# A softmax kernel whose second load is issued as 16 DMAs of unequal partition counts

## The chip, the cores and the metric

The kernel runs on one core of one Trainium2 chip. The metric is the time of the whole program on the device in microseconds (us), the median over runs; lower is better. The span of a profile runs from the first to the last instruction and is about 1.8 us shorter than that. Each experiment was timed on the same chip as a run of the kernel before.

## The reference

```python
x: (16, 1024, 512) float32
def reference(x):
    x_max = np.max(x, axis=-1, keepdims=True)
    exp_x = np.exp(x - x_max)
    return (exp_x / np.sum(exp_x, axis=-1, keepdims=True)).astype(np.float32)
```

It is 33.55 MB in and 33.55 MB out.

## The kernel before

The 16384 rows are cut into ten chunks. Chunk k gives `R` rows to each of the 128 partitions and has a place in one SBUF tile of 96 rows. SyncE issues the loads and ScalarE the stores. VectorE finds the row maxima (reduction) and scales; ScalarE computes the exponentials and their sums. SBUF is the core's on-chip memory, in 128 partitions. A DMA copies between it and DRAM; it *lands* at the last recorded increment of its semaphore, a counter that engines wait for (the trace of the kernel before has 368 increments by DMAs, 16 for each of its 23). In the profile DVE is VectorE, ACT ScalarE, POOL GpSimd, and SPq is SyncE's own list of instructions.

```python
CHUNKS = [
    (3, 0), (5, 3), (8, 8), (16, 16), (16, 32), (16, 48), (16, 64), (16, 80), (16, 0), (16, 16),
]                      # (rows per partition, first SBUF row)
EARLY = 8              # loads 0 to 7 stand first in the program
AFTER_STORE = {2: [8], 3: [9]}
FINISH_BEFORE = (1, 2, 3)
ON_ACT = ()            # loads that ScalarE issues
AT_HEAD = {mybir.EngineType.SP: 1}   # the first load is issued ahead of the start barrier
# ... cut: views, groups of 8 rows ...
    def load(k):
        queue = nc.scalar if k in ON_ACT else nc.sync
        queue.dma_start(out=place[k], in_=src[k])
# ... cut: rowmax and exps ...
    def scale(g):
        # ... cut: reciprocal of the sums, one multiplication per row ...
        if since is not None:
            nc.scalar.dma_start(
                out=dst[k][:, since:b, :], in_=place[k][:, since:b, :]
            )
        if b == CHUNKS[k][0]:
            for later in AFTER_STORE.get(k, ()):
                load(later)
# ... cut ...
        for k in range(EARLY):
            load(k)
        # then per group: rowmax, exps, and the scale of the group before
```

One thing is not in this text. The instruction records of both traces show eight semaphores for these DMAs, numbers 99, 100 and 103 to 108, shared by loads and stores and used in turn: in the trace of the changed kernel the first load has 99, the 16 shares of the second 100, 103, 104, 106, 107, 108, 99, 100, 103, 104, 105, 106, 107, 108, 99, 100, and the first store has the 105 that the first round leaves out, so that the share of 6 gets it after the store. Of the first eight loads, each that gets a used one is recorded with a wait for it: the sixth to eighth in the kernel before. (The stores' records name a wait for VectorE's semaphore, 101, alone.)

Of the kernel before, what the change touches and what calls it, by code (L numbers as in the profile page):

```python
# [1 line left out]

# [4 lines left out]

F32 = mybir.dt.float32
EXP = mybir.ActivationFunctionType.Exp
AX = mybir.AxisListType.X  # L10


CHUNKS = [
    (3, 0), (5, 3), (8, 8), (16, 16), (16, 32), (16, 48), (16, 64), (16, 80), (16, 0), (16, 16),
]
SBUF_ROWS = 96

EARLY = 8
AFTER_STORE = {2: [8], 3: [9]}

GROUP = 8

FINISH_BEFORE = (1, 2, 3)

STORE_ROWS = {3: 8, 4: 8, 5: 8}

ON_ACT = ()

AT_HEAD = {mybir.EngineType.SP: 1}



def loads_at_the_head(nc):

    main, body = nc.main_func.blocks[0], nc.main_func.blocks[1]
    for engine, count in AT_HEAD.items():
        loads = [
            i
            for i in body.instructions
            if i.engine == engine and type(i).__name__ == "InstDMACopy"  # L40
        ][:count]
        barrier = next(
            n
            for n, i in enumerate(main.instructions)
            if i.engine == engine and type(i).__name__ == "InstDrain"
        )
        for load in loads:
            body.instructions.remove(load)
        main.instructions[barrier:barrier] = loads


@with_exitstack
def kernel(
    ctx: ExitStack,
    tc: tile.TileContext,
    x: bass.AP,
    out: bass.AP,
):
    nc = tc.nc
    nc.at_finalize(loads_at_the_head)  # L60
    P = nc.NUM_PARTITIONS

    x_flat = x.flatten_outer_dims()
    out_flat = out.flatten_outer_dims()
    n, d = x_flat.shape
    assert n == P * sum(R for R, _ in CHUNKS)


    src, dst, at = [], [], 0
    for R, _ in CHUNKS:  # L70
        for flat, views in ((x_flat, src), (out_flat, dst)):
            part = flat[at : at + P * R, :]
            views.append(part.rearrange("(p r) d -> p r d", r=R))
        at += P * R

    data = ctx.enter_context(tc.tile_pool(name="data", bufs=1))
    stats = ctx.enter_context(tc.tile_pool(name="stats", bufs=4))
    held = data.tile([P, SBUF_ROWS, d], F32, name="held")
    place = [held[:, s : s + R, :] for R, s in CHUNKS]


    groups = []
    for k, (R, _) in enumerate(CHUNKS):
        m = max(1, round(R / GROUP))
        cuts = [R * i // m for i in range(m + 1)]
        since = 0
        for a, b in zip(cuts, cuts[1:]):
            ends = b == R or b - since >= STORE_ROWS.get(k, R)
            groups.append((k, a, b, since if ends else None))
            since = b if ends else since  # L90
    shift = [None] * len(groups)
    sums = [None] * len(groups)

    def load(k):
        queue = nc.scalar if k in ON_ACT else nc.sync
        queue.dma_start(out=place[k], in_=src[k])

    def rowmax(g):
        k, a, b, _ = groups[g]
        shift[g] = stats.tile([P, b - a], F32, name="shift", tag="shift")  # L100
        nc.vector.reduce_max(  # L101
            out=shift[g], in_=place[k][:, a:b, :], axis=AX, negate=True
        )

    def exps(g):
        k, a, b, _ = groups[g]
        sums[g] = stats.tile([P, b - a], F32, name="sums", tag="sums")
        for r in range(a, b):
            nc.scalar.activation(  # L109
                out=place[k][:, r, :],  # L110
                in_=place[k][:, r, :],
                func=EXP,
                bias=shift[g][:, r - a : r - a + 1],
                scale=1.0,
                accum_out=sums[g][:, r - a : r - a + 1],
            )

    def scale(g):
        k, a, b, since = groups[g]
        recip = stats.tile([P, b - a], F32, name="recip", tag="recip")  # L120
        nc.vector.reciprocal(out=recip, in_=sums[g])  # L121
        for r in range(a, b):
            nc.vector.tensor_scalar_mul(  # L123
                out=place[k][:, r, :],
                in0=place[k][:, r, :],
                scalar1=recip[:, r - a : r - a + 1],
# [9 lines that stand above are left out]
    with tc.manual_schedule():  # L136
        for k in range(EARLY):
            load(k)
        waiting = None
        for g, (k, a, _, _) in enumerate(groups):  # L140
            if waiting is not None and a == 0 and k in FINISH_BEFORE:
                scale(waiting)
                waiting = None
            rowmax(g)
            exps(g)
            if waiting is not None:
                scale(waiting)
            waiting = g
        scale(waiting)


# [1 line left out]
_INS = ['x']  # L153
_OUTS = [((16, 1024, 512), 'float32')]


# [23 lines left out]
```

## Time and profile before

| | before |
|---|---|
| time, median of 2 runs | 162.52 us (161.56 to 163.48) |
| span of the profile | 159.7 us |
| DMA over the span | 67.13 MB, 420 GB/s |
| VectorE busy, ScalarE busy | 78%, 58% |

First, lines of the page of the kernel before. Each digit is the busy share of one fortieth of the span (4.0 us) in tenths, and each number below is that slice's GB/s. The DMA engines are full, or nearly so, from the second slice to the last but one.

```profile
## 2 busy tenths in 40 slices
DVE  0481870799699999999999999999999999762000
...
DMA  7999999899999999999999999999999999999993
GB/s 269 433 464 411 389 447 446 383 412 466 402 441 431 460 435 396 439 418 468 427 414 439 414 484 427 396 447 402 435 439 476 418 402 468 443 402 468 427 410 164
DMA packets 3315, 67.13 MB, mean 420 GB/s; under 512 B 368, under 2 KB 368, under 8 KB 624
```

The same by windows of the kernel before (start and end, length, busy us and instructions (x) of VectorE, ScalarE and GpSimd, granted clock, busy share of the DMA engines, GB/s):

```profile
0.00:5.00 5.00, 0.52 (x1) 0.47 (x1) 0.20 (x4) 1.00 0.81 303
5.00:10.00 5.00, 2.67 (x6) 3.04 (x7) 0.00 (x0) 1.00 0.99 418
10.00:18.00 8.00, 4.27 (x7) 3.63 (x10) 0.00 (x0) 1.00 1.04 430
18.00:32.00 14.00, 8.15 (x12) 5.75 (x16) 0.00 (x0) 1.00 0.99 424
32.00:100.00 68.00, 66.23 (x82) 49.09 (x137) 0.00 (x0) 1.00 1.01 432
```

At 432 GB/s the 67.13 MB take 155 of the 159.7 us, so the DMA engines are the limit: a microsecond in which they have nothing to do is lost unless the end of the kernel had slack, and for DMA it has none by the slices above (8 or 9 tenths from the second to the last but one).

The front of the chain of waits of the kernel before (start us, us, what). It shows the first load landed at 4.46 us and the second reduction following the first scaling at 10.01 us without a wait: the second load was long there.

```profile
0.00 4.46 DMA held<-in_x_dram
4.46 0.02 issue
4.48 1.76 DVE shift L101
...
8.73 1.28 DVE held L123 x3
10.01 2.74 DVE shift L101
```

SyncE's own waits in the first 20 us of the kernel before (waiter and releaser: us in total, times, longest). It waits only for loads:

```profile
SPq L96 <- DMA held<-in_x_dram: 4.3, 2, 2.7
```

### The profile page before, as it was taken

Reading aid. Unit: us, or ns where it says so; the run is one execution under the profiler, and the core shown is the slowest. Engines: PE = TensorE matmul, PEld = TensorE weight load, DVE = VectorE, ACT = ScalarE, POOL = GpSimd, SP = SyncE. Lnnn points to the kernel's source line nnn. Section 1 sums busy time; section 2 is a strip of 40 time slices with the busy share of each in tenths; the row PEclk is TensorE's granted clock in tenths of the full one; section 3 lists DMA queues with packets and bytes.
Section 4 is the critical chain, followed back from the end, with each engine's and each line's share of the span. In section 5 each row is a group of like instructions: output and inputs, shape, how many; then the busy total and the mean of one; then the engine's idle time right before and its main releaser. Section 6 shows DMA issues by size and latency. Waiting matters only on the chain.

```text
span 159.7 us, 521 instructions
## 1 busy us (share of the span) xinstructions
DVE 123.9 (78%) x162; ACT 93.3 (58%) x257; POOL 0.2 (0%) x4
## 2 busy tenths in 40 slices
DVE  0481870799699999999999999999999999762000
ACT  0718129208994959595868677686859595930000
POOL 0000000000000000000000000000000000000000
DMA  7999999899999999999999999999999999999993
GB/s 269 433 464 411 389 447 446 383 412 466 402 441 431 460 435 396 439 418 468 427 414 439 414 484 427 396 447 402 435 439 476 418 402 468 443 402 468 427 410 164
DMA packets 3315, 67.13 MB, mean 420 GB/s; under 512 B 368, under 2 KB 368, under 8 KB 624
## 3 DMA queue, kind: packets, MB, share of 16 engines
q1 hardware_dynamic: 1440, 33.56, 49.5%
q10 hardware_dynamic: 1872, 33.56, 48.9%
q14 instruction: 3, 0.02, 0.0%
HBM read 33.55 MB, written 33.55 MB: 420 GB/s over the span
## 4 chain that ended last, share of the span: by engine, by line
DVE 70%; ACT 14%; issue 3%; DMA 3%; DVEq 0%; ACTq 0%
DVE shift L101 38%; DVE held L123 30%; ACT held L109 14%; DMA held<-in_x_dram 3%; DVE recip L121 2%; DVEq L175 0%; ACTq L109 0%
## 5 line engine op out<-in xcount | busy, mean ns | idle before, releaser
L109 ACT ACTIVATE held<-held,shift 128x512 f32<-128x512 f32 x128 | 90.5, 709 | 43.4 <-DVE shift L101 33.2
L101 DVE TENSOR_REDUCE shift<-held 128x8 f32<-128x4096 f32 (+2 forms) x17 | 70.6, 4161 | 4.5 <-DMA held<-in_x_dram 4.5
L123 DVE TENSOR_SCALAR held<-held,recip 128x512 f32<-128x512 f32 x128 | 52.2, 481 | 0.6
L109 ACT ACTIVATION_READ_ACCUMULATOR held<-held,shift 128x1 f32 x128 | 24.0, 187 | 0.0
L121 DVE RECIPROCAL recip<-sums 128x8 f32<-128x8 f32 (+2 forms) x17 | 3.3, 193 | 15.8 <-ACT held L109 15.8
L109 ACT ACT_TABLE_LOAD x1 | 1.3, 1283 | 4.5 <-DMA held<-in_x_dram 4.5
L164 POOL MEMSET const-bfloat16-1.0<- 128x1 bf16 x1 | 0.1, 102 | 0.0
L164 POOL MEMSET const-uint8-127<- 128x1 uint8 x1 | 0.1, 102 | 0.0
L164 POOL MEMSET const-float32-1.0<- 128x1 f32 x1 | 0.1, 99 | 0.0
L164 POOL MEMSET const-float32-0.0<- 128x1 f32 x1 | 0.1, 98 | 0.2 <-issue 0.2
## 6 DMA issues: line engine op xcount, KB each, us to landing
held<-in_x_dram SPq DMA_DIRECT2D x7, 4096.0 KB, 41.8
out_dram<-held ACTq DMA_DIRECT2D x4, 4096.0 KB, 21.0
out_dram<-held ACTq DMA_DIRECT2D x7, 2048.0 KB, 35.5
held<-in_x_dram SPq DMA_DIRECT2D x1, 2048.0 KB, 11.3
held<-in_x_dram SPq DMA_DIRECT2D x1, 1280.0 KB, 6.7
out_dram<-held ACTq DMA_DIRECT2D x1, 1280.0 KB, 20.0
held<-in_x_dram SPq DMA_DIRECT2D x1, 768.0 KB, 4.5
out_dram<-held ACTq DMA_DIRECT2D x1, 768.0 KB, 15.7
```

The lines of the kernel that those rows point to most:

```text
L101: nc.vector.reduce_max(out=shift[g], in_=place[k][:, a:b, :], axis=AX, negate=True)
L109: nc.scalar.activation(out=place[k][:, r, :], in_=place[k][:, r, :], func=EXP, bias=shift[g][:, r - a : r - a + 1], scale=1.0, accum_out=s ...
L121: nc.vector.reciprocal(out=recip, in_=sums[g])
L123: nc.vector.tensor_scalar_mul(out=place[k][:, r, :], in0=place[k][:, r, :], scalar1=recip[:, r - a : r - a + 1],)
L164: nc = _bacc.Bacc("TRN2", target_bir_lowering=False, num_devices=1)
```

## The change

The intent is not stated. It looks like an attempt to cut one load into unequal shares: one load becomes 16, of 8, 15, 14, ... 1 neighbouring partitions.

```diff
+SHARES = {1: (8, 15, 14, 13, 12, 11, 10, 9, 8, 7, 6, 5, 4, 3, 2, 1)}
 ...
     def load(k):
         queue = nc.scalar if k in ON_ACT else nc.sync
-        queue.dma_start(out=place[k], in_=src[k])
+        p = 0
+        for n in SHARES.get(k, (nc.NUM_PARTITIONS,)):
+            queue.dma_start(out=place[k][p : p + n], in_=src[k][p : p + n])
+            p += n
```

## The prediction

> **What bounds the kernel now.** The DMA engines. The page's slices show DMA at 9 tenths or so from the second slice to the end, and the table by windows 430 to 435 GB/s from 32 to 120 us; 67.1 MB at 432 GB/s is 155 of the 159.7 us. The chain of waits names VectorE (70%), but its last store is issued at 144.8 us, when the store before still needs until 149 us to land (landing records): compute has about 4 us of slack. At the front the first load lands at 4.46 us, the second before VectorE wants it (its reduction starts at 10.01 us, right after the first scaling), and DMA is full from 1 us on.
>
> **What the change does.** Same bytes, same compute in the same order. SyncE issues 16 small DMAs in place of one. The intent is probably unequal shares[...]. The trace has no engine numbers to confirm it. The last store's landings spread over only 1.2 us, so balance can give about 1 us at most.
>
> **The cost.** A load issue takes about 0.33 us, 0.38 us from one to the next. The built program has eight DMA semaphores, handed out in turn to loads and stores alike, and a DMA that reuses one waits for the landing of the DMA that had it. In the changed program six shares go out at once, four wait for DMAs that land early, but the share of 6 partitions waits for the *first store*, issued at 10.04 us after the first scaling. On idle engines I estimate its landing 4.4 us after issue (the first load, of equal size, took 4.46): 14.4 us. The shares of 6 to 1 follow at 0.38 us each; the last is issued at about 16.4 us and lands 1.9 us later (1.0 to the first packet, 0.4 for 10 KB, 0.4 to the semaphore), at 18.3 us. There the second reduction starts: compute is 8.3 us later. The third load (1.16 us before) is issued at about 16.8 us, so DMA is full again only at 17.8 us. Until then it moved 2.9 MB; before, 6.95 MB (360 GB/s for 10 us, then 430). The missing 4.07 MB at 432 GB/s are 9.4 us.
>
> **On the critical path.** All 9.4 us: DMA is saturated to the end before, and afterwards too, as later loads and stores keep a backlog. The 8.3 us of compute hide under it.
>
> **Time.** 162.5 + 9.4 = 172.0 us, 8 in 10 between 169.6 and 174.6. Faster by over 2%: 0.02; within 2%: 0.03; slower: 0.95.
>
> **Right or wrong in the profile.** Right: DMA slices nearly empty from about 6 to 11 and 14 to 17 us; SyncE's waits name a long out_dram<-held wait at the load line; the five-row reduction starts at 17 to 19 us after a DMA wait of about 8 us; about 397 GB/s over the span; DMA busy from there to the end. Wrong: that reduction near 10 us, or idle DMA later.
>
> **What would make it wrong.** Issues[...] costing much more than 0.38 us (up to 175 us) or less; the first store landing sooner[...].

The sum is 162.5 + 9.4 = 172.0 us as recorded. Of the rule on reused semaphores the traces show the part on loads (told above).

## The result, and the profile after

The changed kernel took 173.37 us (172.81 and 173.92), a ratio of 1.0696 with a 95% interval of 1.058 to 1.081. Executions over 1.5% slower than the fastest of the same kernel are left out of the means. Ratios here are those made from fast runs alone; they are not quite the ratio of the medians (here 1.067). A later run of the same kernel in six fast runs gave 173.73 us and 1.071 (1.0675 to 1.0746), beside a median of 162.29 us for the kernel before.

Lines of the page of the changed kernel, in slices of 4.3 us:

```profile
## 2 busy tenths in 40 slices
DVE  0430064914996999999999999999999999945000
...
DMA  7844799999998999999999999989999899999993
GB/s 239 137 106 166 229 471 414 429 412 445 439 422 376 423 483 397 445 441 410 445 448 402 479 414 410 487 385 429 422 429 483 383 475 391 468 414 445 429 429 153
DMA packets 3427, 67.14 MB, mean 393 GB/s; under 512 B 480, under 2 KB 480, under 8 KB 736
```

The loss stands in slices 2 to 5, and nothing later is different. There are 112 packets more, all under 512 bytes. They fit the landing records: in the kernel before, 368 packets under 512 bytes and 368 increments; in the changed kernel, a share of n partitions has n increments where a whole DMA has 16, so that the 16 shares have 128 for 16 before, and that is the 112 more. Each share has one further increment right after its issue (the share of 8 at 1.25 us, its eight others from 4.82 to 6.83 us). How many DMA engines a share runs on, and which, no run shows.

Windows of the changed kernel, columns as before:

```profile
0.00:5.00 5.00, 0.00 (x0) 0.00 (x0) 0.20 (x4) 1.00 0.79 231
5.00:10.00 5.00, 1.78 (x2) 3.50 (x7) 0.00 (x0) 1.00 0.68 113
10.00:18.00 8.00, 1.43 (x4) 0.00 (x0) 0.00 (x0) 1.00 0.44 138
18.00:32.00 14.00, 6.61 (x8) 3.63 (x10) 0.00 (x0) 1.00 1.01 412
32.00:100.00 68.00, 60.45 (x72) 45.88 (x128) 0.00 (x0) 1.00 1.00 426
```

From these rows: by 18 us the changed kernel moved 2.82 MB and the kernel before 7.05 MB. Counting the DMA packets of both traces by their ends, the changed kernel reaches 2.8 MB 9.3 us later, 3 MB 11.1 us later, 30 MB 11.0 us later and 65 MB 10.8 us later. So everything is lost in the first 20 us and nothing is given back: that is what a saturated resource looks like. I call this distance at 30 MB the DMA lag below. It is good to about half a microsecond: the control below has 0.4.

The front of the chain of waits of the changed kernel:

```profile
0.00 5.91 DMA held<-in_x_dram
...
10.19 1.29 DVE held L128 x3
11.47 0.02 issue
11.49 4.07 DMA out_dram<-held
15.56 0.02 issue
15.58 0.27 SPq L100
...
16.88 0.25 SPq L100
17.14 0.04 issue
17.18 4.40 DMA held<-in_x_dram
...
21.66 2.83 DVE shift L106
```

This is the chain in order: a *load* line (SPq L100) is released by the landing of a *store*. The second reduction starts at 21.66 us in place of 10.01. SyncE's waits in the first 20 us of the changed kernel say the same:

```profile
SPq L100 <- DMA out_dram<-held: 7.9, 1, 7.9
SPq L100 <- DMA held<-in_x_dram: 3.8, 4, 2.8
```

The first line of that chain holds something that was not expected: the first load, which the change doesn't touch, lands at 5.91 us in place of 4.46. Only the last three of its 16 landings are late (4.66, 5.53 and 5.91 us; before 4.07, 4.44 and 4.46); the other 13 come by 3.74, before by 4.00. And the 128 packets of 10,240 bytes of the second load took a median of 901 ns each, where the kernel before has 385 ns.

### The profile page after: what moved, and what is told of

It is laid out like the page before. It is cut to its first block, busy times and chain, and to the rows that moved or that the text cites. A ratio compares the mean times of both kernels' runs of the same rounds, so it can differ in the third digit from the quotient of the medians.

```text
span 171.0 us, 540 instructions
## 1 busy us (share of the span) xinstructions
DVE 124.0 (72%) x162; ACT 93.3 (55%) x257; POOL 0.2 (0%) x4
## 4 chain that ended last, share of the span: by engine, by line
DVE 67%; ACT 13%; DMA 8%; issue 2%; SPq 1%; DVEq 0%; ACTq 0%
DVE shift L106 37%; DVE held L128 28%; ACT held L114 13%; DMA held<-in_x_dram 6%; DMA out_dram<-held 2%; DVE recip L126 1%; SPq L100 1%; DVEq L180 0%; DVEq L106 0%; ACTq L114 0%
```

## The experiments

Two questions. Is the wait for the first store the cause (the theory of the prediction), or the small DMAs themselves? And why are the packets slow? A theory for the second, called *crowding* below: DMAs of a few neighbouring partitions slow each other when they are in flight together, and partitions that lie apart do so less. It was a guess, and the runs below test it by time alone: where such partitions would get in each other's way, no trace shows. Rivals: fewer completions per DMA (n in place of 16), the number of issues, or the unequal shares.

| run | what | time us | ratio (95%) | DMA lag us |
|---|---|---|---|---|
| the change, again | | 173.73 | 1.071 (1.068 to 1.075) | 10.9 |
| wait_alone_mended | wait, no shares | 171.50 | 1.058 (1.055 to 1.061) | 9.7 |
| shares_no_wait | shares, no wait | 171.34 | 1.056 (1.049 to 1.062) | 8.0 |
| spread_no_wait | spread shares, no wait | 169.18 | 1.042 (1.038 to 1.046) | 6.9 |
| spread_wait | spread shares, wait | 174.08 | 1.074 (1.069 to 1.080) | 11.3 |
| eight_neighbours | 8 equal shares of neighbours | 167.21 | 1.029 (1.025 to 1.034) | 4.7 |
| eight_spread | 8 equal shares, spread | 164.29 | 1.012 (1.008 to 1.017) | 2.0 |
| sixteen_columns | 16 DMAs of all partitions | 165.77 | 1.021 (1.017 to 1.025) | 4.1 |
| before_store_pool | control | 162.15 | 0.999 (0.995 to 1.004) | 0.4 |

The runs of the kernel before beside them had medians of 162.06 to 162.29 us. The DMA lag of every run is against the first profile of the kernel before.

### wait_alone: built wrongly

```diff
-    (3, 0), (5, 3), (8, 8), ...
+    (3, 0), (5, 0), (8, 8), ...
```

> Kernel before, with the second chunk put into the SBUF rows of the first: its load (one DMA, 128 partitions) now waits for the landing of the first store, as the share of 6 partitions does in the changed kernel, and every later load stands behind it on SyncE. No small DMAs, no uneven shares. Theory (the semaphore wait for the first store is the cost): first store issued near 10.0 us, landed near 14.1; second load issued then, third near 14.8; until 15.4 us about 1.57 MB moved where before moved 5.5 MB, so about +9 us, ratio 1.055. Rivals (many issues,[...] uneven shares are the cost): within 1% of before.

It took 177.39 us (1.093) and its results were wrong (relative error 0.21). All loads stand before all compute in the program, so the second load overwrote the first chunk as soon as that had landed, and not after its store. The kernel tests nothing of the theory.

### wait_alone_mended: the wait without the shares

```diff
-    (3, 0), (5, 3), (8, 8), ...
+    (3, 0), (5, 0), (8, 8), ...
-EARLY = 8
-AFTER_STORE = {2: [8], 3: [9]}
+EARLY = 1
+AFTER_STORE = {0: [1, 2, 3, 4, 5, 6, 7], 2: [8], 3: [9]}
```

> The first wait_alone was built wrongly (its second load overwrote the first chunk). Here the loads after the first stand after the first store in the program, and the second chunk uses the rows of the first, so the second load, one whole DMA, waits for the landing of the first store and the others stand behind it. Right results. The wait alone, as in the prediction: store issued near 10.0 us, landed near 14.0; second load then, third near 14.5; DMA full from about 15.1 us with 1.57 MB moved where before had moved 5.4 MB: +8.9 us, ratio 1.055. If the wait costs little without crowded shares: under +4 us.

Correct, 171.50 us, ratio 1.058: 9.3 us over the 162.15 of its rounds, where 8.9 was expected. SyncE's waits in its first 20 us, and two of its windows:

```profile
SPq L96 <- DMA out_dram<-held: 12.5, 1, 12.5
```

```profile
5.00:10.00 5.00, 2.53 (x5) 2.88 (x7) 0.00 (x0) 1.00 0.00 0
10.00:15.00 5.00, 0.00 (x0) 0.00 (x0) 0.00 (x0) 1.00 0.57 190
```

No byte moves for 5 us. So a wait of this kind, with whole DMAs and nothing else changed in the load, is *enough* for a loss of 9 us. It doesn't follow that the wait is all that the change does, nor that the same wait costs as much there: here nothing of the second load moves until the store has landed (in the change 107 of its 128 partitions, 1.1 MB, do), and the store lands sooner, at 13.18 us in place of 15.56.

### shares_no_wait, and its control

The first store goes to GpSimd's queue; no share waits for a store any more (SyncE's waits below).

```diff
-            nc.scalar.dma_start(
+            (nc.gpsimd if k == 0 else nc.scalar).dma_start(
```

> Changed kernel with the first store alone issued on GpSimd's queue[...], so that no share waits for a store; the 16 shares stay as they are. If the wait is the whole cost: within 1% of before. If shares of neighbouring partitions are slow by themselves (packets of 10 KB took about 1.0 us in the changed kernel, 0.385 before; about 120 GB/s), the wait only hid it: shares landed by about 14 us, third load issued near 12.8, DMA full near 14.3 us with about 2.7 MB moved where before had moved 5.0 MB, so +5 to +6.5 us, ratio 1.03 to 1.04.

> Control: kernel before with its first store on GpSimd's queue. All theories: within 0.5% of before; if it is not, the two runs above have to be read against this one.

The control is unchanged at 0.999. The changed kernel without the wait still takes 171.34 us, ratio 1.056, more than both expectations: taking the wait away gains only about 2 us. SyncE's waits in its first 20 us, then three of its windows:

```profile
SPq L100 <- DMA held<-in_x_dram: 10.0, 13, 2.8
```

```profile
5.00:10.00 5.00, 1.75 (x1) 3.15 (x6) 0.00 (x0) 1.00 0.65 100
10.00:15.00 5.00, 1.46 (x4) 0.35 (x2) 0.66 (x1) 1.00 0.62 174
15.00:25.00 10.00, 3.69 (x4) 3.63 (x10) 0.00 (x0) 1.00 1.05 431
```

The store's wait is gone, and SyncE waits 13 times for landings of the first load and of earlier shares instead, because the 16 shares go round the eight semaphores told above. The shares move at 100 GB/s, with the DMA engines busy for 0.65 of the time (packets again about 0.9 us), so those landings are late; the third load is issued at 13.55 us in place of 1.16. And a new cost shows at the end: the last store's 16 landings are spread over 3.3 us (165.45 to 168.71), against 1.18 before and 1.39 in the change. Its last landing is 9.85 us later than before's (158.86), though its DMA lag is 8.0. The unequal shares may be the cause, but the run doesn't isolate it, and spread_no_wait below, with the same sizes and no wait either, has a spread of only 1.68 us. Why the change itself has so little is not shown.

### eight_neighbours and eight_spread: crowding by itself

```diff
-SHARES = {1: (8, 15, 14, 13, 12, 11, 10, 9, 8, 7, 6, 5, 4, 3, 2, 1)}
+SHARES = {1: (16,) * 8}
 # eight_spread alone, in load(k), cut: partitions 8 apart, r counts the DMAs
-            queue.dma_start(out=place[k][p : p + n], in_=src[k][p : p + n])
+            rows = slice(r, r + 8 * (n - 1) + 1, 8)
+            queue.dma_start(out=place[k][rows], in_=src[k][rows])
```

> Second load as 8 equal DMAs of 16 neighbouring partitions:[...] 8 issues, no load that holds data back waits for the store. Measures crowding alone. [...]packets of 10 KB about 1.0 us, shares landed near 11 to 13 us, +4 to +8 us. If only the number of small DMAs or uneven shares cost: under +1 us.

> As eight_neighbours with the 16 partitions of each DMA 8 apart[...]. Crowding theory: packets near 0.5 us, +1 to +3 us, clearly less than eight_neighbours. Rival: the same as eight_neighbours.

(The first figures of eight_neighbours are those of the crowding theory.)

Both have equal shares, with 16 landings each, and the same issues and waits in the same order. The neighbours cost 4.9 us (167.21 over 162.29), the spread ones 2.0. The windows of eight_neighbours, then of eight_spread:

```profile
5.00:10.00 5.00, 1.75 (x1) 3.51 (x7) 0.00 (x0) 1.00 1.02 152
10.00:15.00 5.00, 2.75 (x5) 0.00 (x0) 0.00 (x0) 1.00 0.97 308
```

```profile
5.00:10.00 5.00, 2.57 (x4) 3.50 (x7) 0.00 (x0) 1.00 1.02 253
10.00:15.00 5.00, 3.37 (x3) 1.60 (x5) 0.00 (x0) 1.00 1.01 431
```

Look at the DMA share: it is 1.02 in both first rows, at 152 and 253 GB/s. A slow packet counts as busy for as long as it takes, so GB/s and not the busy tenths tells how much DMA does. The median 10 KB packet took 1061 ns with neighbours, 719 ns spread, and 385 ns in one DMA of 128 partitions. With 16 landings and equal shares in both, neither fewer completions nor unequal shares are needed for the slowness. The order is that of the crowding theory, and the only change between the first two is which partitions go together. Their DRAM rows change with them, so a part played by the DRAM side isn't excluded; where the packets were held up was not observed. The first load shows the same order: it lands at 4.30 to 4.50 us in every run whose second load is not cut by partitions, at 4.93 to 5.30 us in those with spread partitions, and at 5.76 to 6.32 us in those with neighbours (third_on_act, with the third load beside it, has 5.29).

### spread_no_wait and spread_wait

The same 16 sizes in the same order, with the partitions of a share 8 apart (15 and 1, 14 and 2, ... fill one class of 16 each), without the store's wait (by the edit of shares_no_wait) and with it. Part of load(k) is cut:

```diff
+        taken = [0] * 8
+        for n in SHARES[k]:
+            r = next(r for r in range(8) if taken[r] in (0, 16 - n))
+            first = r + 8 * taken[r]
+            rows = slice(first, first + 8 * (n - 1) + 1, 8)
+            queue.dma_start(out=place[k][rows], in_=src[k][rows])
+            taken[r] += n
```

> As shares_no_wait, and the partitions of each share lie 8 apart[...]; same sizes, same order, same semaphores. If crowding[...] is what slowed the shares: packets of 10 KB nearer 0.5 us than 1.0[...]; DMA full near 10.2 us, so +3 to +4.5 us, ratio 1.02 to 1.03, clearly under shares_no_wait. If small DMAs are slow for another reason (HBM side, issue[...]): the same as shares_no_wait.

> Changed kernel with the partitions of each share 8 apart[...]; first store on ScalarE's queue as before, so the share of 6 still waits for it. Theory (the wait decides, crowding only delays the first load's last landing by 1.4 us and the refill): first load landed nearer 4.5 than 5.9 us, first store landed near 14.4, +9 to +10 us, ratio 1.055 to 1.062, that is 1 to 2 us less than the changed kernel. If crowding is the main cost: +4 us or less.

Without the wait: 169.18 us, ratio 1.042, clearly less than shares_no_wait (1.056) but more than expected. With it: 174.08, ratio 1.074, no better than the change, a miss. Packets did get faster (median 571 and 548 ns) and the first load of spread_wait landed at 4.93 us. What ate the gain in spread_wait, by its trace, is the issue. This line of the timeline of spread_wait (start us, us, what) has ten issues in 7.84 us:

```profile
0.78 7.84 SPq L106 DMA_DIRECT2D held<-in_x_dram  x10
```

An issue of a share of two or more partitions 8 apart held SyncE for 0.60 to 0.86 us, where the change has 0.25 to 0.38. The six after the store's landing then took from 13.84 to 17.84 us, so the third load came no sooner than in the change (17.48). These two runs therefore mix two effects; eight_neighbours and eight_spread are the cleaner pair, and there too the spread issues were the dearer ones (0.49 to 0.59 against 0.31 to 0.42 us).

### sixteen_columns: the number of issues

```diff
+        whole, given = place[k].rearrange("p r d -> p (r d)"), src[k].rearrange("p r d -> p (r d)")
+        for c in range(0, 2560, 160):
+            queue.dma_start(out=whole[:, c : c + 160], in_=given[:, c : c + 160])
```

> Second load as 16 DMAs of all 128 partitions and 160 columns each (640 bytes): the same number of issues and of reused semaphores,[...] and in the built program no load of the front waits for the store. Costs of issuing alone: 16 issues at 0.35 to 0.4 us put the third load near 7 to 8.5 us while the DMA engines have only 2.1 MB to move until then, so +1.5 to +4 us, ratio 1.01 to 1.025. If the number of issues made the change slow by itself: +8 us or more.

165.77 us, ratio 1.021, 3.5 us over the 162.29, in the expected range. The timeline of sixteen_columns shows the 16 issues and when the next load got its turn:

```profile
0.78 7.86 SPq L103 DMA_DIRECT2D held<-in_x_dram  x16
8.68 2.04 SPq L99 DMA_DIRECT2D held<-in_x_dram  x4
```

Every DMA here covers all partitions (16 landings each) and no load of the front waits for a store; what is left is SyncE's time and the small packets. The run doesn't separate these two: a packet of 640 bytes took 32 ns at the median, 20 GB/s where one of 10,240 bytes in 385 ns has 27, and from 4 to 12 us the DMA engines were busy for 0.66 to 1.13 of the time and moved 170 to 233 GB/s. So the 3.5 us are a measure of both, not of the issues alone.

### third_on_act: more work for the DMA engines during the wait

```diff
-ON_ACT = ()
+ON_ACT = (2,)
```

> Changed kernel, and its third load (2 MB) is issued by ScalarE at the start, so that the DMA engines have 2.1 MB more to move while SyncE waits for the first store. If idle DMA engines are what costs: the DMA lag falls from about 10.8 to about 6 us. Compute still starts its second chunk near 21.5 us, so its last store is issued near 156.5 us and can't land before about 167.6: +6 to +9 us, ratio 1.04 to 1.055, with the last store no longer queued behind the one before it. If idle DMA is not the cause: no change, +11 us.

177.69 us, ratio 1.095: a miss in the other direction. Moving the load shifted the round of semaphores by one in the built program, so that the share of 11 now waits for the *third load*, and that load, in flight together with the crowded shares, needs 16.92 us. Its chain of waits has that landing, at 17.69 us, before the next share's issue:

```profile
0.77 16.92 DMA held<-in_x_dram
...
17.71 0.29 SPq L100
```

The DMA lag is 12.7 us, and the time is 15.5 us over before: here compute is so late (the second reduction starts at 29.02 us) that its last store, issued at 163.86 us, finds the DMA engines idle (busy share 0.06 from 160 to 163.8 us). So compute hides under DMA only as long as its delay doesn't outgrow the lag of the DMA by more than the few microseconds of slack.

### skew_late: unequal shares late in the kernel

```diff
-SHARES = {1: (8, 15, 14, 13, 12, 11, 10, 9, 8, 7, 6, 5, 4, 3, 2, 1)}
+SHARES = {6: (120, 8)}
```

> Kernel before, with the 16-row load of chunk 6, deep in the backlog, issued as 120 and 8 partitions[...]. Imbalance theory: nothing absorbs it there,[...] +0.5 to +1.3 us, ratio 1.003 to 1.008. If bytes are rebalanced over engines by the hardware: ratio 1.000.

174.43 us, the median of its four fast runs, ratio 1.077 (1.073 to 1.081), where at most 1.008 was expected. One of the last store's 16 landings comes at 161.65 us and the other 15 from 170.4 to 172.9: they are uneven to the end, as expected. But most of the loss is elsewhere. Windows of skew_late:

```profile
20.00:40.00 20.00, 14.15 (x12) 9.11 (x25) 0.00 (x0) 1.00 1.01 429
40.00:60.00 20.00, 18.41 (x27) 15.71 (x45) 0.00 (x0) 1.00 1.03 358
60.00:80.00 20.00, 16.76 (x24) 15.32 (x44) 0.00 (x0) 1.00 0.98 242
80.00:100.00 20.00, 18.62 (x21) 9.83 (x27) 0.00 (x0) 1.00 1.00 429
```

The DMA of 120 partitions has 15 landings, and they come from 71.8 to 75.4 us; the one of 8 partitions lands at 81.2 us. From 52 to 72 us the rate is 272 GB/s at a busy share of 1.01, with a median of 2.1 us for a packet of 32 KB where the kernel before has 1.21 (the row of 60 to 80 us holds parts of both DMAs): the mark of the crowded shares again. In what order its partitions moved isn't visible, so crowding as the cause is not shown. As a measure of imbalance alone the run failed.

### change_again

A comment apart, the changed kernel.

> The changed kernel itself, unchanged, for a tighter interval and a second trace. If crowding adds to the wait (first load's last landing near 5.9 us in place of 4.4, refill after the shares slower): 172.5 to 173.5 us, ratio 1.066 to 1.071, that is 1 to 2 us above wait_alone_mended, with the first load's last landing again near 5.9 us and packets of 10 KB near 0.9 us. If the wait alone explains everything: ratio 1.058.

173.73 us, ratio 1.071; the first load's last landing at 5.76 us, packets at a median of 823 ns. Its interval lies wholly above that of wait_alone_mended. So the change loses some 2 us more than that run. How the 11.4 us divide between the wait and the shares isn't shown, as the wait of that run is not quite the same (above).

## Why the prediction was right

The time of 172.0 us and its range held (173.37). Point by point:

- *DMA is the bound and stays saturated afterwards.* Right. The lag is complete at 20 us and is 10.8 to 11.1 us at 3, 30 and 65 MB.
- *The share of 6 waits for the first store.* Right, and it was read from the waits of the built program, not from the diff. The changed kernel's chain has the load released by the store at 15.56 us, after 7.9 us of SyncE's waiting. wait_alone_mended shows that such a wait alone costs 9.3 us, where the prediction had 9.4 for the whole change. That these two agree so well is luck, as they are different sums: there the store lands at 14.4 us and 1.1 MB of shares have moved before, here it lands at 13.18 us and none have.
- *Balance gains at most about 1 us.* No gain is seen: the last store's landings spread over 1.39 us (1.67 in change_again), 1.18 before.
- *The waits for landings of the early shares don't matter; small DMAs are as fast as a whole one.* Wrong. This step was left out of the sum. It was hidden, as those transfers ran during the wait for the store, which the prediction did not foresee and so had by luck: without that wait the shares still cost 9.3 us (shares_no_wait). The two costs are nearly alternatives and don't add up: 9.3 each, about 11.4 together.

The terms of the sum (us from the start, or for; the last row counts from its issue):

| term | predicted | measured |
|---|---|---|
| first load landed | 4.46 | 5.91 |
| first store issued | 10.04 | 11.49 |
| first store, issue to landing | 4.4 | 4.07 |
| from that landing to the third load's issue | 2.4 | 1.9 |
| third load issued | 16.8 | 17.48 |
| 3 MB moved | 18.0 | 20.0 |
| lag of DMA | 9.4 | 10.8 to 11.0 |
| second reduction starts | 18.3 | 21.66 |
| last share's landing | 1.9 | 4.40 |

(The predicted 18.0 for 3 MB is 2.9 MB at 17.8 us and 432 GB/s from there.) The mis-sized terms are the first and the refill. The shares delayed the end of the first load (likely by crowding); that made the store 1.45 us later. Cheaper issues and a slightly quicker store gave part back. "DMA is full again only at 17.8 us" was too early: lag at 2.8 MB was 9.3 us, almost the prediction, and grew to 11.1 within the next 0.2 MB. In that stretch the third load's packets (16 KB) took up to 1.65 us where their usual time is 0.61.

The last share took 4.40 us and not 1.9, probably because an estimate for one packet was used. The trace has a run of six packets of 10 KB, each starting within 3 ns of the end of the one before it, from 16.47 to 20.57 us, and the last increment comes 1.0 us after that, at 21.58. Which engine served them the trace doesn't say. The lost 11.65 us of compute stayed under the lag plus the slack, so this error cost the prediction nothing. Also wrong in detail: DMA was not "nearly empty" from 6 to 11 us, it moved 113 GB/s from 5 to 10 us and called itself 68% busy; and the reduction began after 19 us, outside the 17 to 19 foreseen.

## What to carry to other kernels

Before you split a DMA, list the waits of the built program: here semaphores used in turn made a load wait 7.9 us for a store, which is nowhere in the text, and with DMA as the bound the idle time came back as total time (9.3 us in wait_alone_mended). Several DMAs of a few neighbouring partitions in flight together were slow here (10 KB packets at 0.8 to 1.06 us in place of 0.385) and slowed the load in flight with them (landed at 5.76 to 6.32 us in place of 4.46); read GB/s beside the busy share, as slow packets look busy. When one cause is hidden behind another, removing the one that the chain of waits names may gain little: run each of them alone before you repair.
